# One shared tile for the fillers of a row, and a new written-out order, in a four-layer trunk on one core

## The chip, the cores and the metric

The kernel runs on one core of one Trainium2 chip. The metric is the device time of one execution in microseconds (us). The core's engines work side by side, each through its own queue in order: PE (TensorE, matrix products; PEld is its loading of weights), DVE (VectorE), ACT (ScalarE), POOL (GpSimd) and SP, which here only issues transfers (DMA) from and to the chip's memory.

## The reference

A residual trunk of four layers over 256 tokens of width 1024, each a token mixer followed by a SwiGLU FFN of inner width 2816. Layers 0 and 3 mix with the recurrent RWKV-7 form, layer 1 with stick-breaking attention, layer 2 with sparse attention over 64 selected keys.

```python
for i in range(DEPTH):                     # DEPTH = 4
    kind, j = i % 3, i // 3
    h = rms_norm(x, norm_mix[i])
    if kind == 0:   y, v_layer = rwkv7_time_mix(h, v_first, ...)   # a scan over the tokens, 16 heads of 64
    elif kind == 1: y = stick_breaking_attention(h, sb_w_qkv[j], sb_w_out[j])
    else:           y = dsa_attention(h, ds_w_in[j], ...)
    x = x + y
    x = x + swiglu(rms_norm(x, norm_ffn[i]), ffn_w_gu[i], ffn_w_down[i])
```

All of it is in float32.

## The kernel before

The residual x lies transposed in four tiles `xt` (128 channels x 2 x 256 tokens each). Weights come as 397 pieces of 128 x 1024 float32 (512 KB). Each is loaded into one of three buffers `raw` (`piece`, L639), cast on ACT or DVE to a rounded half `wh`, and DVE forms the rest `wl` = raw − wh; products are then sums of passes with `wh` and `wl`. Where the program takes unsplit float32, as in the sums of squares `ss` and the LoRA products `lora_in`, a matmul instruction shows as two records in the profile.

The first recurrent layer begins like this (`prep_chunk` L732, `rwkv` L890): the four parts of x are loaded; ACT squares them and DVE adds; four matmuls with ones make the sums over channels (`ss`); ACT and DVE make 1/rms of them (`rstda`, `rstdm`, `rstd`). The LoRA input weights, the first 512 KB of `lora`, are scaled on DVE (`mu`, `lora`), and PE multiplies x by them (`lora_in`). When rstd is there, DVE makes the normed h and its mixtures (`pre`, `xm`), these are split into `kx`, and PE starts the key projection (`kp`). A second transfer of 1.5 MB brings the rest of `lora`, which `lw` and `la` read first.

Nothing here is issued in program order. `Plan` records all 6561 operations with their dependencies. The text `ORDER` (L302) holds, packed, the order in which they are issued, the engine of each operation that could run on more than one (801 of them), and the buffer slot of each tile; a search made it, with a planner's costs (`_cost`, L253). `schedule` (L481) unpacks it, and `emit` (L529) issues the operations in that order, each into its engine's queue. All are thereby recorded at one line, L560.

An entry of the order that names no operation is a **filler**: work for PE without use, whose place the search chose. `emit` looks for a PSUM slot that no product holds (`held`) and calls `warmer` with it; `warmer` (L1607) then issues two matmuls (`WARMERS`, L220) of 256 columns of ones in bf16, `warm_x`. Each of the two matmuls takes a new tile `warm_o` in that slot. A slot has one buffer (`bufs=1`), so a new tile in it stands for the end of the one before.

Of the kernel before, what the change touches and what calls it, by code (L numbers as in the profile page):

```python
# [15 lines left out]
F32 = mybir.dt.float32  # L16
# [39 lines left out]
_o = 0  # L56
# [163 lines left out]
WARMERS = 2  # L220
# [87 lines left out]
SA;iomc0Icd(#bMS4_wDlD%R5V>9F>OIN-
5{Ey0cUC*`sd|prIbRko*GrAaOLQDFp%w;Y3^Q@DX+4v7Lf8aSXwxxD`i#xtuu&rDyB>#YOU%W5mmjsvM=~HftXPooLoL}62z%MvIr>i@h?w#>desIQ*IX
~q4e2)nDXn*T`^NRBWeo22D{DiOd==oXib9{G$kIv8e;ssImR`3>f5nFTE#(%;lV!b}V`fly-v5ytR5@G>y9<x8p;!HJ0j4-4-A!ZS64;`dW%aRI<-  # L310
)Pl^rE;Yz$AWevq3+uvj6^^m-
+AtpU6e&D?_$=;#<8EtWPrQ(0_OY3TqbO039cCvQVgc1PUK&`^%fK2knw%S*zVUE+ZnMDb*lr`?=v>f*4EgX%T`xbnceHLWs7weaCT0yE^E)UJFLT5qt$F
MR%ec!U18-;f2qStE!IVr7qwQd$tqb^D?x?X`H<xSvYuiYX3u#HKv_)c40YxZJW>~W3}R5QDa%Z-
0(Tnxi?*&=Y$jAYN;Ey`9x+F86@c<?domUoYc_(gZArc0X?0PPcE^^b75PxhysScHExVtEVtZ6<#c<Kc>_dH>jl$J%r3vR@xL7aF@6NNrJAR(!z=h5lMOf
2;2jM1^ydrbm+>*<jejLN+X8CGlS)fndX$`eiMT6_bGN>YWZ+qM=g2R`<s^Z+b*7|m_HwuCPF0<CAa=}qPJhX%Zig#C|C|cer>H@#WtG@E~s_@8lVd$X8t
O{dKEeN)?q>!hWhbPh!Lq{lU^Vo{3N~o(68A3{^KNI$zsPGUP3PCvQjw6_LWdY(5S_d1JWr+_~G%8DJ4)-
M66O3~JwngG;xKc_D73s4n)xJ_7uOyITfKuxqB@+W6-v$AkuW-N-
;w1uc?i1@H1=~_e4dS_kJt1gR93U{_g3%RSP@io8;66U4zVRjo&&(_eM#L!LJq29sC5%HuEa55eQNq|KXCTfe_<zs&_~$q;UvfSqgMcvF8v@P{mYDHUq7!
g5R*^1_u|a`sE*NaVYfLOQ1mM%R2N^mBU~Vrn2<al{nTO#5<mhCc!cy8zWL*>x6XdWU9eHKK4@sA9`iYdwP^4Q?);#c*fntk-huX4&oRI`WBMGuO_WA%5S
$e4~`9zjz2>DDV8LI^z#R3sp6rnVfLo$W3O~<_4kXh+TaE8dajy35js5ecZZv@5z0x`r|h<H#oQ@fi9<bdX$KnHk>y1+nG$WDqkBp@dhBZz$<ogA14$8sN  # L320
# [48 lines left out]
"""


class Plan:
# [156 lines left out]
    def emit(self, nc, counts, warmer):  # L529
# [15 lines left out]
        for b in left:  # L545
            for o in b.ops:
                of[o].append(b)
        for n, o in enumerate(ops):
            if o is None:
                free = [(at, tag) for tag, (at, b) in held.items() if b is None]  # L550
                if free:
                    warmer(min(free)[1])
                continue
            for b in of[o]:
                left[b].discard(o)
                held[b.slot] = (n, b if left[b] else None)
            if not o.instrs:
                nc.scalar.preload_act_table_set(o.table)
            for method, args, kw in o.instrs:
                getattr(getattr(nc, o.eng), method)(*map(real, args), **{k: real(a) for k, a in kw.items()})  # L560
# [1042 lines left out]

    wx = sb.tile([P, S], BF16, name="warm_x")
    nc.vector.memset(wx, 1.0)
    plan.emit(nc, {"ps": 6, "g": 2, "xm": XMS, "raw": RAWS, "wh": 3, "wl": 3, "t": TS, "t2": 5},
              lambda tag: [nc.tensor.matmul(psum.tile([P, 512], F32, name="warm_o", tag=tag, bufs=1)[:, :S], wx[:, :P], wx, start=True, stop=True)  # L1607
                           for _ in range(WARMERS)])

# [159 lines left out]
```

## Time and profile before

| | us |
|---|---|
| time, median of 3 runs (lowest, highest) | 1365.79 (1365.06, 1367.98) |
| profiled execution | 1365.3 |
| its span, first to last instruction | 1363.5 |
| PE busy | 1353.9 |
| DVE busy | 1131.2 |
| ACT busy | 728.2 |
| PE busy with fillers (46 matmuls) | 16.3 |

The profile shows one execution. Times in it count from the start of the span. A row of a timeline has the start, the duration, the engine, the line, the operation, what it writes and reads, and how many instructions are merged in it; in brackets stands for how long the engine was idle before, and what ended that. `x8` for a float32 product means four instructions. Matmuls overlap in the pipeline, so the distance between starts tells the rate, not the duration.

The stages follow one another on PE: recurrent layer 0 to 196 us, its FFN to 379, stick-breaking to 500, FFN to 678, sparse attention to 820, FFN to 998, recurrent layer 1 to 1177, FFN to the end.

### The profile page before, as it was taken

Reading aid. Unit: us, or ns where it says so; the run is one execution under the profiler, and the core shown is the slowest. Engines: PE = TensorE matmul, PEld = TensorE weight load, DVE = VectorE, ACT = ScalarE, POOL = GpSimd, SP = SyncE. Lnnn points to the kernel's source line nnn. Section 1 sums busy time; section 2 is a strip of 40 time slices with the busy share of each in tenths; the row PEclk is TensorE's granted clock in tenths of the full one; section 3 lists DMA queues with packets and bytes.
Section 4 is the critical chain, followed back from the end, with each engine's and each line's share of the span. In section 5 each row is a group of like instructions: output and inputs, shape, how many; then the busy total and the mean of one; then the engine's idle time right before and its main releaser. Section 6 shows DMA issues by size and latency. Waiting matters only on the chain.

```text
span 1363.5 us, 25718 instructions
## 1 busy us (share of the span) xinstructions
PE 1353.9 (99%) x10380; PEld 1183.0 (87%) x10380; DVE 1131.2 (83%) x1913; ACT 728.2 (53%) x1245; POOL 8.3 (1%) x18
## 2 busy tenths in 40 slices
PE   9999999999999999999999999999999999999998
PEld 5888798888888898888899798888898888988888
DVE  5999799876688899876799989877699997998754
ACT  3765465654344655654346866554148564656532
POOL 0000000000000000000000000000000000000000
PEclk9999999999999999999999999999999999999999
DMA  5524157664655356655646546666653331666554
GB/s 181 169 88 126 34 154 219 200 194 145 186 175 165 113 185 202 203 176 163 199 155 184 157 140 216 204 196 203 187 153 111 111 98 34 199 206 199 174 172 132
DMA packets 62999, 221.89 MB, mean 163 GB/s; under 512 B 7328, under 2 KB 8864, under 8 KB 62624
## 3 DMA queue, kind: packets, MB, share of 16 engines
q1 hardware_dynamic: 62880, 220.25, 52.4%
q8 instruction: 81, 1.33, 0.4%
q14 instruction: 38, 0.31, 0.1%
HBM read 217.08 MB, written 1.05 MB: 160 GB/s over the span
## 4 chain that ended last, share of the span: by engine, by line
PE 98%; DVE 1%; DMA 1%; issue 0%; ACT 0%; DVEq 0%; SPq 0%
PE gate L560 18%; PE up L560 18%; PE dn L560 18%; PE po L560 7%; PE qk L560 6%; PE vp L560 4%; PE rp L560 3%; PE vps L560 3%; PE kp L560 3%; PE z L560 2%; PE warm_o L1607 1%; PE sc L560 1%; PE Y L560 1%; PE cmb L560 1%; PE pg L560 1%; PE attn_o L560 1%
## 5 line engine op out<-in xcount | busy, mean ns | idle before, releaser
L560 DVE TENSOR_TENSOR wl<-raw,wh 128x1024 fp32r<-128x1024 f32 x285 | 347.3, 1221 | 85.3 <-ACT wh L560 82.2
L560 ACT CAST wh<-raw 128x1024 fp32r<-128x1024 f32 x219 | 229.3, 1049 | 179.2 <-PE dn L560 92.4
L560 PE MATMUL dn<-h,wh 128*128 128x512 f32 (+1 forms) x726 | 244.3, 383 | 0.0
L560 PE MATMUL dn<-h,wl 128*128 128x256 f32 x704 | 198.1, 282 | 0.0
L560 PEld LDWEIGHTS dn<-h,wh 128*128 128x128 f32 x726 | 134.7, 188 | 26.9
L560 PE MATMUL up<-xg,wring 128*128 128x512 f32 x704 | 139.8, 336 | 0.0
L560 PE MATMUL gate<-xg,wring 128*128 128x512 f32 x704 | 138.3, 336 | 0.0
L560 PEld LDWEIGHTS dn<-h,wl 128*128 128x128 f32 x704 | 133.0, 189 | 0.0
L560 DVE TENSOR_TENSOR wring<-raw,wring 128x1024 fp32r<-128x1024 f32 x88 | 107.5, 1222 | 28.9 <-ACT wring L560 27.9
L560 PE MATMUL gate<-xg,wh 128*128 128x512 f32 x352 | 126.8, 392 | 0.0
L560 PE MATMUL up<-xg,wh 128*128 128x512 f32 x352 | 126.5, 392 | 0.0
L560 PEld LDWEIGHTS gate<-xg,wring 128*128 128x128 f32 x704 | 107.5, 188 | 14.7
L560 PEld LDWEIGHTS up<-xg,wring 128*128 128x128 f32 x704 | 107.4, 188 | 14.6
L560 ACT CAST wring<-raw 128x1024 fp32r<-128x1024 f32 x76 | 79.9, 1051 | 35.8 <-issue 15.3
L560 PE MATMUL up<-xg,wl 128*128 128x256 f32 x352 | 98.4, 280 | 0.0
L560 PE MATMUL gate<-xg,wl 128*128 128x256 f32 x352 | 98.4, 279 | 0.0
L560 PE MATMUL qk<-xg,wh 128*128 128x256 f32 (+1 forms) x384 | 91.8, 320 | 0.0
L560 PEld LDWEIGHTS up<-xg,wh 128*128 128x128 f32 x352 | 66.1, 188 | 14.5
L560 PEld LDWEIGHTS gate<-xg,wh 128*128 128x128 f32 x352 | 66.1, 188 | 14.5
L560 PE MATMUL qk<-xg,wl 128*128 128x256 f32 x256 | 71.7, 280 | 0.0
L560 PEld LDWEIGHTS qk<-xg,wh 128*128 128x128 f32 x384 | 63.8, 189 | 6.2 <-issue 0.5
L560 ACT COPY gus<-gate 128x256 f32<-128x256 f32 x88 | 32.3, 373 | 68.9 <-PE gate L560 66.8
(325 smaller groups left out, 2663.9 us busy)
## 6 DMA issues: line engine op xcount, KB each, us to landing
raw<-in_wts_dram SPq DMA_DIRECT2D x397, 512.0 KB, 3.8
lora<-in_lora_dram SPq DMA_DIRECT2D x2, 1536.0 KB, 9.0
rhl<-qa SPq DMA_DIRECT2D x32, 64.0 KB, 3.4
xt<-in_xT_dram SPq DMA_DIRECT2D x4, 256.0 KB, 3.6
lora<-in_lora_dram SPq DMA_DIRECT2D x2, 512.0 KB, 5.7
lg<-in_lora_dram SPq DMA_DIRECT2D x8, 128.0 KB, 3.6
inv<-in_id_dram SPq DMA_DIRECT2D x2, 512.0 KB, 4.0
out_dram<-xt SPq DMA_DIRECT2D x3, 256.0 KB, 4.5
```

Of the source, the lines that this page charges most:

```text
L560: getattr(getattr(nc, o.eng), method)(*map(real, args), **{k: real(a) for k, a in kw.items()})
L1607: lambda tag: [nc.tensor.matmul(psum.tile([P, 512], F32, name="warm_o", tag=tag, bufs=1)[:, :S], wx[:, :P], wx, start=True, stop=True) for ...
```

## The change

There are two parts.

**Fillers in a row share one tile.** `emit` keeps the tile of the last filler. The next filler writes the same tile again, as long as no product has taken the slot in between. The two matmuls of one filler share it too. `warmer` takes the tile where it has one.

**A new order.** The packed text is replaced. It keeps all 6561 operations. Unpacked, the two texts compare as follows.

| | before | after |
|---|---|---|
| entries | 6584 | 6595 |
| fillers | 23 | 34 |
| fillers ahead of the first `ss` | 19 | 27 |
| other fillers on PE, in runs | 2, 1, 1 | 1, 1, 2, 1, 2 |
| operations on DVE | 1896 | 1899 |
| operations on ACT | 1208 | 1205 |

The order within the sparse attention layer is the same on every engine. In the two recurrent layers and in stick-breaking attention it changes on PE, DVE, ACT and SP, in the FFNs at their ends, mostly. Operations that change engines: 29 from DVE to ACT and 29 back in recurrent layer 0, 25 and 17 in stick-breaking attention, 21 and 23 in recurrent layer 1, 31 in all in the FFNs. Many buffer slots change.

The head of SP's queue, where the first layer starts:

```
before: xt1 xt0 xt2 xt3 vecs lora(512 KB) raw raw raw raw consts raw lora(1.5 MB) raw raw raw ...
after:  xt0 xt1 xt2 raw vecs xt3 lora(512 KB) raw raw raw lora(1.5 MB) raw raw raw raw raw consts ...
```

On ACT, the cast of the first weight piece moves from behind `rstd` to ahead of the squares of `xt3`, and DVE's split of that piece to ahead of the scaling of `lora`.

```diff
@@ -300,72 +300,75 @@
 ORDER = """
-c-rk+S#KoCab{%XRd-ca-xvELn`iTEcC&eN$>ChfA$NvzXm+*I>{{}!4qLKy*cJ=}h5*}u{9qV<Fkr|Jda(RzKgcisBmM=3U_gJsfFrBAIWwAFOSWWK3oz
...
+c-rk+*>9xVQFqnZzrA<2?cUvXyWMWPSFbZ3d+Zr|#-
...
 """
@@ -545,15 +548,20 @@
         for b in left:
             for o in b.ops:
                 of[o].append(b)
+        filler = None
         for n, o in enumerate(ops):
             if o is None:
                 free = [(at, tag) for tag, (at, b) in held.items() if b is None]
-                if free:
-                    warmer(min(free)[1])
+                if filler is None and free:
+                    filler = min(free)[1], warmer(min(free)[1])
+                if filler is not None:
+                    warmer(*filler)
                 continue
             for b in of[o]:
                 left[b].discard(o)
                 held[b.slot] = (n, b if left[b] else None)
+                if filler is not None and filler[0] == b.slot:
+                    filler = None
             if not o.instrs:
                 nc.scalar.preload_act_table_set(o.table)
@@ -1603,9 +1611,15 @@
     wx = sb.tile([P, S], BF16, name="warm_x")
     nc.vector.memset(wx, 1.0)
+
+    def warmer(tag, t=None):
+        if t is None:
+            return psum.tile([P, 512], F32, name="warm_o", tag=tag, bufs=1)
+        for _ in range(WARMERS):
+            nc.tensor.matmul(t[:, :S], wx[:, :P], wx, start=True, stop=True)
+
     plan.emit(nc, {"ps": 6, "g": 2, "xm": XMS, "raw": RAWS, "wh": 3, "wl": 3, "t": TS, "t2": 5},
-              lambda tag: [nc.tensor.matmul(psum.tile([P, 512], F32, name="warm_o", tag=tag, bufs=1)[:, :S], wx[:, :P], wx, start=True, stop=True)
-                           for _ in range(WARMERS)])
+              warmer)
```

More of the change, by code (lines that the diff above doesn't have):

```diff
@@ L308 @@
[L308 to L320, printed above, removed]
@@ new lines @@
+Ub6zb|cMIR~y@h(to#Q)2cPm}+ouTj=u5XUap*!xlgUH!6E!V$e_M1azAzWTI-Eln|ICTg3(%*!-q!-
+kmsGsD+;*Z@zO|f*@q;jSj$#lU;Cf(ncWGjQd_zmSmeAQD@My~pnqrNHKue)4G;Yg00A@>AhMxc5_aQ^&ld;{4Fj(Bl=j*synzKw|Y>2rK^f_QuP&L_Bc8
++Q?R5bu6%YY&O!0ta;S7&q_`KkVX5JYHEn!uAE;!4`JUaIl29jMzl1#y{o1!f^@bNa$?g&v7uD$2?+s>EF|sqDL5@j~F;<%=;dqpHk>xRVaaZUSV@Nk@+>
+57oLmR)cg5#ikr7WFAyL4oEKfk&*x1Jvu+k=vVNMUJsx4mBzgk5QTm+Coa=`YrM%x)bp6qxL`>~-WP5yfPjKAc=38_(!eL{G!@&@--
+*+n;=+xJ+)52AT&6ZqVMA5`rgI8-<VOT<m&F-
+AQIu@`}Y39pV%He!D%e+~JvknFUW_rw{O@=<22sJC1b;W4U8u^e3R$z3K(Ku4`r0cBku=*i)c*&rajO}<;;S!S;MHS$-
@@ new lines @@
+FFo$6h#!P9sB7tA*_F=7IiH)G6IFqmD!;&UJc}82KgTdr!7>JY4CmIvVkN}F-NO7b**n*HSz!4U=A=s*Oz)*qSiw-OsQHhUl~?q3XOF#51mkQFG~I_iQ53
+V)*|3eyS&o}#$E4A;a@8F6vkx@-
+s?x!*RO(~?G%tMAs}w>e(C5)cRP5?mT|o5C%|@o#&A4fKQA0DTV6&|Kb@b+f5uW=6*W2K;*#c}jPaS9IH~}{=g24EC$Xu10(`;6%wx1j4z&n#}529!*58<
+OM)6nx~70BljTqQv34Xr`ZSr0*}9>GUr=H>1T!y^|R2k3oI6TwrHj1A-a(DCHhbzL}jz_^?)Z37zBx`GoD>VmUO&-
+%uk8gSMel48zG&ln%pJZbqJJ3zOVaW!V#P;e?i5Mzs;4UBm}kGnDBxs_v}n=n3cfNr@4(}@{-
+3LX%n0LN*8A<l>NcwJk@M^=u3bsaN4bzl%PD$}7YVPC;RNu0o)6=EEcf?y3njF0KgSTRx&<Anpmgi)<o#(`ZiX5?*R9GUw>+CwrM=u;vB8SBGQK{KYSavH
@@ new lines @@
+F087jco!Y(857?bjl5OR75m`0%C(<cq9bPep&HH3)fbb@q^+BBh&qE9ED%9NxPRs{hmrw|N)@B!9IK+F&Eltf!_Kv;v>m^ovYS%W;pO98AY$XPuZ4{1q8`
+17iOsV?0_mwc>CY76q|bk@GClhU3CZVH^xy2}cvlv1IZC5sHgtO_VcD3zyIQcHTSR7Kq*E78_xdBiI`;9&~c>>jgb=sRdAhFeGy5oiX=vuI{S9ytnz=^}<
+?tbq39uegMqhGJQ-
+=_*GGe4JzW<cMQ6&&oNL&6*7AFQqUVWFSn1TOUVJ7=rM7%gdzn4;H;f!>iw0S~^;)*WvpOc2cibYpenXo8@u&oli!i^6(48tzl*Gt<m7^;czfO=q+qKJKZ
+?hcndyQKi)W!r`<zw@5#M`<Aaw+M+bKgP7h)B&dHs9eq31b_TMRayWYq1ovp=ecEmSZZehqb$~;&9UdJ3|Lq5A4@LNs)yT`l{90oNmeptD6E4LTz?na^*Z
+i?~a&L|kJ4ubamr)_OoKhVp3Y3cS7KbDK|hk}WH7`+Wc7?ihO_WS)(?}xg-@n*00Qm@bd08i?jx#RFi-L14*xO^L6uj#(Kv*Yf5ac+liZ*CR83?nlH-ADB
@@ new lines @@
+x183dh+U!xclXfMT0FIhFO|CZGO;y`@=C`VQ{py{K+&W}Exti|DqO)9zPMzlB_M(%kk8-
+u30AH$59kJj;O3xPxI?RPUOQ;gLy+x39!;S@vQGorSe_H_OYJnV~h>Wwx4l5hApoNkze6fiHDg$YDW%yhN&>0EONw<IiPVNM&TY>gl@(qt7O@JED@?n{m#
+2(DQm}ih46D*ha$}h`1`BJF_?<}-&1;E?$Alz;=puP`FU#a14HI3zT=|FuorEW(m)PaBlf*1mc5KiZq4+YGNgPbrKq2Jdc+fss%tw9LC<-
+lFfkgpP41c8QU3Mi!t?(c#pnL{RR8H&a?WrH#$H#kb|>wyjlIxajU(}L!txhq-Q5EN5R-
+DpTjMj0JZ7%o#Ba^AVec??8I$UA{Ei?BTnCuA{h+T$3Z&NKtLCefnKxy70_3pKPpA>o;sAmP|zDDg@QQO+~MEI!aNP{o`BIJe>76+&!-
+^Mpc;Ji;b~3uTg3VorK@0TUctC;d?kCu@?rgb$mB02c-
@@ new lines @@
+A*Fn^F@2m4+2Q0*P?T`CQ5bGfL+_So&`d%Kv!FJ-9&{A5jc+i#6ON`1k=@~<-)$m|#DA7wxM5Eg6IXPJx2)9T5|8<n?Q?GYf(iT&!rA!6a4yv<;*-
+pcE(GY!StqlS9>acb@8EUK#UJK@SOD)pm<aB=hxYQ7$9pYQaVZKvB@t_J>gJ}UUCxUy5;_-k+%ie-pa7Ti2GN3a;MmRI}Hk5j6_Gc`Z8#L|mVO0<7Ba+fR
+FLbxEnFM8=PHTNA;Bp<;a$zO$xFbWEiV&EgS0t6+`QM}>3*BCsh=W0-
+WoLxH2mZ6>zaG26ZcMf#nOy`3JsI8}4TPj!CPE&OC7O|h|M!FN`PYCOLky=bQ3ZfZRoiM`*Y$FyHA<PCY@Vk0GWJcB58f61&$T(2pg^mpt>I_KOEP6F@<g
+&6OmBy1sfVTWsj>FDbxK8+;lkKdZ>523Msy;iRG^*^u`JgEl#T<3tRG*aLAzxtK`Ai+!=`;??a8`=e7ih32nE@+;zg}2eT*Qk;9&0%8E4@l3lY#N$H0a0)
@@ new lines @@
+Hz=h2bcT<<?xhAPG4IYn@t&aaL-(=^)J&{3VD%`45b{8ZU>$0;V}F%<thDdKeTS-
+N2;Mc2U6vW;q~N|0qD)qCM3<t|lPm6FCPN9~!7XFfgMhzJf>&&xhWAubzK6CrB^VH^LMgO}E!Ko^nbR7__4NaTpw?_5dv2k3gAmk(XO6}Cev&3Sgp^eE%7
+@phURy86eSvvm?=CrQmKY|W-KC0;I6<BzjH|$GMxkWXkJ0{VEa!S=8hxJpq9MslpC`W%NMGd_o2p;UFA}Eth3;O-
+FU0s+`9;Dszr>86KfmD0Yw}C|Q~8A@1poPJhWR&|{_7IJzra5;=CZU+K#L^6wJ(<}U1(=37T!74)tqO5EfEpKiD=d44RR;4fbB3K&KtIq&e`9*PT3=BGb=
+V?)H1cnM<|O>;iB1!B0y(UItNrHWE@Ie8ko<7NQ*Y@%q~T-lF4UymZx~srQ4kEXSnC_HJ56+jN>e%$lV-
+#80AbDvikv}jgpt8sMrX&;&N*kH%?RwvW`t>G**F-
@@ new lines @@
+l8jO=leY6+MFy97Nr9dPE;vLX1Q+19r~wJ6#g~x*qwi>TTf?4$oq*k<Cc_zq;*WqS<~q#qN57+)OZMQn>kZI{^xZT&VvklG{3>>#-
+C1E@royb%Py?#YstxHfRawB&n*kJ!e*&&=phGn+=H<Kq>ML}`_W*sJQ<~vA8Idv~2mFs!gsv-
+>`?k&5lcJ^!MJ>;Gx+r;Qj)ebZu3Y{w6gjT9J$>kMHB>EsIi-2NBmN$1wEOZV8{a9hu*T<>SvOTGvYKf9X}*$oO9FDH2#_hLR9Jv02Yx709-
+V`ia=cHRsN*`3_g(%8dB$&fbox?r$!$p?ZSHqDqrgNe9X>#OkHg~!c<&71<<Tje0NjJe0C&mYcj$8qU>6=d19%_y-
+i3EyXAH+fI2jM9=jioe<MAOCD+B1l=Egm8s`u8~OVEbpR-gQ_R)+?)RnUNctc<K%E(}UUxj0WxTBLmw@_#WV_AC`RiSPOm{291u@^#l}GOV>;&Q|#~P16=
+HF;!N@8WqK|7^-}cV6pJQR|HTf^2q&|OAjLQ*1Ujh_JTutX#SE@vS0xVd~y;=-TdJU`N&W7jGo~XY1WMn#lZo&EA>>cJD}JF+}gBp2(-n1-
@@ new lines @@
+dY8o?T|U<yU$C8x>ZssnEWz0%Vq9iSjAM5I~ipIs*$F<_J{^EYDb$R7%And`nK=2R4J-
+u#PpME5uhT53ddT9msTMM@(^@<`rsdZ1$>vSB2q(dnz`jjTL~Y)a1-A?=KaAWCm9xI3)u7X|?fZ=$Eie7sqRI;x&_1E`=tf*L1s7W4a<-
+t^m_re1<Nsx7c*I@vGP=Kc)4jm@kbrvC&lTt0yp3?{YRZ=%pR6O<vg?ex?Ta3jMWXfX_I1+ks!1>UCyd>}Rb6S3lE#c)1anYzqLd@BNyAt{Lr`lfh@7(Wl
+3!|70oN{0xbqV$e=Gn;fP6wt?A5q2sjiMO(Aw7J!gc+JK-aLP2Dl@;XXkIpXggh(^%Na<a)LY*<cwf=#T<1;wphlrA(Uq0GiDr-
+z&goJ2B_b9=RWXK`2xE)n8~a>8uaA`Lmx#J-@aR$4l$a_!gtNV<_ev>8rING@m_bdl0B3Qd)ouqZk~*!T<+43WgIBsI8JF12)$I5}F?NH`Z-NMy-jC3|9t
@@ new lines @@
+$tK}rg$RY98MnKRcLA|~u*s>>Z&Jt#w5CZO@##woKx{&0*QedSN;dJ1pNGtzSgb?*GMSMMSM$j%p@@&`a+V-$vQsvhT@IW)r9-qk7CbpGb}30<;zt-CT%r
+xe=8Hj_2-
+uV$e$A#fpfgBF?5#b9IK22oU3(JjDiT=ocEUe}F>4QYT~VuKoH=6^?Q66L0TW#krxlYZwD)mb!~}Bc!Hgvb{(nK1oEJm9HY1MdJkfHp^~v;d#xJLM_3&!Y
+Gs(35ss;sK`bB)0f&$mpB+SNzhQw&LqKKWEP3>Um1zawNleH%xVdY=?FGbQ+3B0c4lqXr8G$x>-
+W<c9I$A+e)T~M?VnIIgYWKNM~VMQ~kL~Jmms+QuO(_30Ob|KBJ`C^E<<^fkmPvY{*ORWlY@HQMdyNXd}m5XBr<M6f0C2kT+;+WVy_6<2TvzP?&|B_6^t4`
+oxI*YfI%%@sG0>Nwoq?2&GoK8G#3d=DJPp~ZUpeqEA&y~k8K`wySqOo@}`&Sk!QN(5e@{JhT@iHDK0nM(=%wk6oR*3Z*E5`nxpmkgs7qSy1w9smKB}<M(#
@@ L369 @@
+%CrhhfODxI=ICPn?GU)vV9n-AVqTU1iBV8h?`z%!fj#yCWNw&MPs{DyB%r22SEE@HFR%L-sXU$%$s6kVj-
+f}(t5eIhmtk|n1vH=mmuM4QhKmU^T8#e$IpZ&%g7jh<TP6(#+afPn<fL61dhBs2zEurrot1U|6{T%n7szLKRpw#!E<>zi$j2>{{^dFD)I
 """
```

68 lines of the change are left out of this document (15 added, 53 removed).

## The prediction

> **What bounds the kernel now.** I read the page first: the busy times and the chain that ended last.
>
> ```profile
> span 1363.5 us, 25718 instructions
> PE 1353.9 (99%) x10380; PEld 1183.0 (87%) x10380; DVE 1131.2 (83%) x1913; ACT 728.2 (53%) x1245; POOL 8.3 (1%) x18
> ...
> PE 98%; DVE 1%; DMA 1%; issue 0%; ACT 0%; DVEq 0%; SPq 0%
> ```
>
> TensorE is the bound, with 9.6 us idle (1363.5 − 1353.9). A reordering that leaves its instructions alone can win only idle time, or PE time in which nothing useful runs. So next: what PE waited for, and the busy time by stretch (columns: length, then busy time and count for PE, PEld, DVE, ACT, POOL; granted clock, DMA share, GB/s).
>
> ```profile
> PE warm_o L1607 <- DVE warm_x L1605: 1.2, 1, 1.2
> PE pS L560 <- DVE Sn L560: 0.7, 2, 0.5
> PE lw L560 <- DMA lora<-in_lora_dram: 0.5, 1, 0.5
> PE vb L560 <- ACT ysq L560: 0.5, 1, 0.5
> ```
>
> ```profile
> 0.00:17.43 17.43, 14.12 (x38) 3.91 (x38) 5.21 (x13) 4.87 (x6) 0.89 (x6) 1.00 0.55 189
> 17.43:27.39 9.96, 9.96 (x40) 8.57 (x41) 5.47 (x11) 5.20 (x8) 0.00 (x0) 1.00 0.13 38
> 27.39:196.00 168.61, 167.04 (x2083) 146.04 (x2082) 155.24 (x311) 100.47 (x181) 3.67 (x5) 1.00 0.39 121
> 196.00:379.00 183.00, 183.00 (x1058) 161.50 (x1057) 144.22 (x202) 91.98 (x139) 0.00 (x0) 1.00 0.61 187
> 379.00:500.00 121.00, 120.92 (x805) 105.37 (x804) 104.35 (x183) 63.45 (x125) 0.40 (x1) 1.00 0.49 154
> 998.00:1177.00 179.00, 177.98 (x2159) 155.03 (x2159) 165.62 (x322) 107.45 (x197) 3.04 (x4) 1.00 0.33 103
> ```
>
> The stretches are: start, lora_in, rest of recurrent layer 0, its FFN, stick-breaking, recurrent layer 1. After 27.39 us PE idles 1.57 us in the first recurrent layer (168.61 − 167.04), 0.08 in stick-breaking, 1.02 in the second: 2.7 us in all. Only the first stretch looks different: there 38 matmuls fill 17.43 us. So, its timeline on PE:
>
> ```profile
> 1.20 16.18 PE L1607 MATMUL warm_o<-warm_x 128*128 128x256 bf16 x38 [1.20 <-DVE warm_x L1605]
> 17.43 3.40 PE L560 MATMUL ss<-sq,ones 128*128 128x256 f32 x8
> 20.68 7.07 PE L560 MATMUL lora_in<-xt,lora 128*128 128x256 f32 x32
> 27.39 0.79 PE L560 MATMUL kp<-kx,wh 128*128 128x256 f32 x2
> ...
> 41.05 9.46 PE L560 MATMUL kp<-kx,ahead 128*128 128x256 f32 x78
> ```
>
> ```profile
> 1.65 0.10 PEld L1607 LDWEIGHTS <-warm_x 128*128 128x128 bf16 x1 [0.32 <-issue]
> ```
>
> The fillers (warm_o) stand 16.23/38 = 0.427 us apart, while a 256-column matmul of kp takes 9.46/78 = 0.12: before each filler's weight load the engine sits 0.32 us on "issue", a wait the profile puts down to nobody. Each of them has a tile of its own. Was PE needed sooner? On ACT and DVE:
>
> ```profile
> 8.20 0.42 ACT L560 ACTIVATE sq<-xt 128x256 f32<-128x256 f32 x1 [2.11 <-DMA xt<-in_xT_dram]
> ...
> 20.88 0.47 ACT L560 ACTIVATE rstda<-ss,eps_rms 128x256 f32<-128x256 f32 x1 [10.96 <-PE ss L560]
> ...
> 22.15 1.03 ACT L560 CAST wh<-raw 128x1024 fp32r<-128x1024 f32 x1
> ```
>
> ```profile
> 8.93 0.42 DVE L560 TENSOR_TENSOR sq<-xt 128x256 f32<-128x256 f32 x1
> 9.95 2.51 DVE L560 TENSOR_TENSOR lora<-lora,mu 128x512 f32<-128x512 f32 x4 [0.60 <-DMA lora<-in_lora_dram]
> ...
> 21.38 0.42 DVE L560 TENSOR_SCALAR rstdm<-ss 128x256 f32<-128x256 f32 x1 [8.92 <-ACT rstda L560]
> ...
> 23.60 1.22 DVE L560 TENSOR_TENSOR wl<-raw,wh 128x1024 fp32r<-128x1024 f32 x1
> ...
> 27.34 0.41 DVE L560 TENSOR_TENSOR kx<-xm,kx 128x256 fp32r<-128x256 f32 x1
> ```
>
> ss had its last input at 9.35 us and began at 17.43: **8.1 us of the start are fillers and nothing else**, with ACT waiting 10.96 us behind them.
>
> **The change, part by part.** The order text, unpacked as `schedule` (L481) unpacks it, has 19 fillers ahead of ss before and 27 after.
>
> 1. *Start fillers.* After, 54 matmuls write one tile. If they stream: the rate doubles once PE has worked densely. ss starts 3.25/8 = 0.41 us apart (17.43 to 20.68), lora_in 6.71/32 = 0.21 (20.68 to 27.39; the same kind, two records to an instruction), a ratio of 1.94, so the switch came some 3.25 us after the first unbroken work, although the clock column says 1.00 throughout. A filler then takes 0.12 warm, 0.23 cold: 14 cold in 3.25 us, 40 warm in 4.8, end at 1.20 + 8.05 = 9.25 us. Never warm: 54 × 0.23, end at 13.6.
>
>    The Trainium skill ("TensorE: Matmul & The Clock Gate", Part 1) lets the clock up only after a busy window of about 3.4 us, and lets the windows run freely, so up to two may pass; the 3.25 us above agree with one. By it, as an estimate, 30 fillers could be cold and the end 10.9.
>
> 2. *ss itself.* The new order issues xT's fourth part behind the first weight piece and the vectors instead of right behind the third, and ACT casts that piece (1.03 us) before the last two squares. SP's queue now:
>
> ```profile
> 0.75 1.81 SPq L560 DMA_DIRECT2D xt<-in_xT_dram  x4
> 2.60 0.43 SPq L560 DMA_DIRECT2D vecs<-in_vecs_dram  x1
> 3.07 0.43 SPq L560 DMA_DIRECT2D lora<-in_lora_dram  x1
> 3.55 21.63 SPq L560 DMA_DIRECT2D raw<-in_wts_dram  x4
> ...
> 27.81 0.43 SPq L560 DMA_DIRECT2D lora<-in_lora_dram  x1
> ```
>
> ```profile
> 27.00:37.00 10.00, 9.47 (x78) 8.99 (x77) 9.92 (x24) 4.56 (x7) 1.13 (x1) 1.00 0.97 346
> ```
>
>    0.65 MB more ahead of it at 346 GB/s is 1.9 us: last square after 10.1, two ACT squares of 0.42 end near 10.6. The cast waits for a piece that is ahead of xT's part, and lies in its shadow. So ss starts at 10.6, between 9.4 (nothing lost) and 13.6 (cold fillers). It is warm: 8 × 0.21 = 1.7, end 12.3.
>
> 3. *lora_in* needs the scaled LoRA weights, ready at 12.46 now (9.95 + 2.51). Their transfer moves behind 0.5 MB more (1.4 us), so the first half is scaled near 12.6 and the rest near 13.9, faster than PE reads it. lora_in runs 12.6 to 19.3. DVE meanwhile goes from ss to the first kx: 27.75 − 20.83 = 6.9 us now, less the 1.2 us weight split that moved ahead of it; kx stands at about 18.1. So **kp starts at 19.3 instead of 27.39: 8.1 us earlier**; by the bounds 9.6 (ss at 9.4) or 5.4 (ss at 13.6).
>
> 4. *Does the rest follow?* After kp's start PE, DVE and SP do the same work in both orders. In 27 to 37 us DVE is busy 9.92 of 10 and the DMA engines 97%, so neither could be squeezed, but both are free earlier: DVE does nothing from 12.5 to 21.4, and DMA carries 38 GB/s in 17.43 to 27.39. The large LoRA transfer, issued at 27.81 behind waits for weight buffers, is issued after the fourth weight piece in the new order; it passes the constants and one weight piece, which then land up to 4.3 us (1.5 MB at 346 GB/s) later against it, but in a time when DMA is idle now. It also ends the 0.5 us for which PE waits for it now. The first constants move back behind five weight pieces; their first user on PE is kss, 40 us on:
>
> ```profile
> L560 PE MATMUL kss<-ksq,consts x8: 590/592/595, 71.6 to 80.9; 128*128 128x512 f32 x8
> ```
>
> 5. *Other fillers:* 4 before, in 3 runs; 7 after, in 5.
>
> ```profile
> 153.17 1.26 PE L1607 MATMUL warm_o<-warm_x 128*128 128x256 bf16 x4
> ...
> 154.58 0.41 PE L560 MATMUL xu<-QC,XT 64*64 64x64 f32 x7
> ```
>
> ```profile
> 1130.31 0.61 PE L1607 MATMUL warm_o<-warm_x 128*128 128x256 bf16 x2
> 1130.98 1.01 PEld L560 LDWEIGHTS cmb<-xd,SB 32*64 32x64 f32 x32 [0.56 <-PE warm_o L1607]
> ```
>
>    A run of one costs 0.67 us, the run of two 1.41: 2.75 in all. After, streamed, a run of one saves some 0.2 (0.45), a further filler costs 0.24: 5 × 0.45 + 2 × 0.24 = 2.7. I take 0; if the old runs covered waits and the new ones do not, +2.7, and −2.7 the other way round.
>
> 6. *The order of the three layers.* PE's instructions are the same. 29 operations go from DVE to ACT and 29 back in layer 0, 25 and 17 in stick-breaking, 21 and 23 in layer 1: DVE's sums hardly move and stay below the stretch (155 of 169, 104 of 121, 166 of 179), so PE hides them; without that cover each costs at most a cast of 1.0 us. At best the new order removes the 2.7 us of PE idle, at worst each waiting place adds about 0.35 (pS: 0.7 in 2). I take −0.8 (the LoRA wait and a little), from −2.7 to +5.
>
> Sum: −8.1 + 0 − 0.8 = **−8.9**, span 1354.6. The profiled execution took 1365.3 us, 1.8 more than its span, and the median of the runs lies 0.5 above it: 1354.6 + 1.8 + 0.5 = **1357 us**. Its own range is 1353.5 to 1360.5: 9.6 instead of 8.1 at the start and all 2.7 us of idle gained below (1.5 + 1.9), 5.4 instead of 8.1 and 0.8 not gained above (2.7 + 0.8).
>
> **Rivals.**
>
> - *The start is held up by something else* (the fourth part of xT, or fillers that stay cold). For: xT is issued later. Against: 3.3 MB move in the first stretch (189 GB/s × 17.43 us), of which xT is 1 MB. Gain 5.4 or less: 1360.5 to 1363.
> - *The waits in the layers go too.* 2.7 us of idle and part of the fillers' 2.7: 1365.8 − 8.1 − 2.7 − 2.2 = 1353, and down to 1350. For: the layers were ordered anew. Against: PE idles so little that a search has hardly anything to find.
> - *Slower: the change does not do what it says.* If the wait before each filler comes from writing the same bank and not from the tile's release, 54 × 0.427 = 23.1 us, end at 24.3, everything 6.8 us later: 1372.6. It decides from a spacing of 16.23/54 = 0.30 us. For: "issue" names no releaser. Against: kp's matmuls write one bank after another without any wait, though they accumulate.
> - *The new order loses in the layers what the start wins.* 23 new waits of 0.35 us, or DVE late in a recurrent layer, where it is busy 92%: 1363 to 1369. For: over 140 of some 335 DVE operations of each recurrent layer move. Against: the old order shows three such waits in 1363 us, beside the first filler's.
>
> **How the numbers follow.** Forecast 0.66, held-up start 0.12, more gain 0.08, fillers still waiting 0.07, lost in the layers 0.07. 0.2% (2.7 us) is about what a measurement tells from no change. Below 1363.1: 0.66 + 0.12 + 0.08 = 0.86. The last case splits mostly into "same" (0.06), the fourth is slower (0.08 with what is left). 1352.5 to 1363.5 leaves out the fourth, most of the fifth and half of the third, about 0.16.
>
> **What would show it.** The new timeline on PE: 54 fillers less than 0.25 us apart, ss near 10.6 and warm from its first record (under 2 us for 8), lora_in done near 19.3, kp 8 us earlier. ACT's wait before rstda shrinks from 10.96 to about 2. Later landmarks, such as the start of the first dn, shifted by the same 8 to 9 us:
>
> ```profile
> 318.36 61.03 PE dn L560 x352
> ```
>
> A shift that shrinks from layer to layer shows part 6 wrong, one that grows the third case. Fillers 0.4 us apart would make the prediction wrong at its root; so would an ss that starts after 14 us.

## The result, and the profile after

| | before | after |
|---|---|---|
| median of the runs, us (lowest, highest) | 1366.88 (1365.06, 1368.37) | 1356.72 (1356.41, 1357.60) |
| ratio, with its 95% interval | | 0.9927 (0.991 to 0.9944) |
| profiled execution, us | 1365.3 | 1356.47 |
| its span, us | 1363.5 | 1354.7 |

The change makes the kernel faster: 8.8 us by the profiled executions, 10.2 us by the medians. The two differ because executions of the kernel before spread more, from 1364.5 to 1373.5 us over all comparisons below, half of them at a lower mean TensorE clock, while those of the changed kernel stay within 1355.8 to 1357.9. The forecast had put the chance on faster, at 1357 us.

The page of the kernel after, its span and busy times:

```profile
span 1354.7 us, 25715 instructions
PE 1347.6 (99%) x10402; PEld 1185.3 (87%) x10402; DVE 1135.6 (84%) x1916; ACT 721.5 (53%) x1241; POOL 8.3 (1%) x18
```

PE is busy 6.3 us less (1353.9 before), though it issues 22 instructions more: the fillers were added, and yet cost less. Its idle time fell from 9.6 to 7.1 us (1354.7 − 1347.6). The start of its timeline, in the columns of the prediction:

```profile
1.20 8.53 PE L1619 MATMUL warm_o<-warm_x 128*128 128x256 bf16 x54 [1.20 <-DVE warm_x L1613]
...
9.78 1.99 PE L568 MATMUL ss<-sq,ones 128*128 128x256 f32 x8
...
11.81 0.47 ACT L568 ACTIVATE rstda<-ss,eps_rms 128x256 f32<-128x256 f32 x1 [1.63 <-PE ss L568]
12.07 7.17 PE L568 MATMUL lora_in<-xt,lora 128*128 128x256 f32 x32 [0.29 <-DVE lora L568]
...
18.89 0.59 PE L568 MATMUL kp<-kx,wh 128*128 128x256 f32 x2
19.32 0.28 PE L568 MATMUL kp<-kx,wl 128*128 128x256 f32 x1
```

54 fillers now stand 8.53/54 = 0.158 us apart, where 38 stood 0.427 apart. ss begins at 9.78 instead of 17.43, ACT waits 1.63 us for it instead of 10.96, and kp begins at 18.89 instead of 27.39: 8.5 us earlier. Whether this lasts is read from the down products of the FFNs. Their tile view names the first start and the last. Before, then after:

```profile
L560 PE MATMUL dn<-h,wh x726: 277/390/392, 318.2 to 1359.5; 128*128 128x512 f32 x171, 128*128 128x256 f32 x11
```

```profile
L568 PE MATMUL dn<-h,wh x726: 277/390/392, 309.1 to 1350.7; 128*128 128x512 f32 x171, 128*128 128x256 f32 x11
```

The first starts 9.1 us earlier, the last 8.8. Nearly all of the gain is there after the first 19 us; from there to the first dn 0.6 are added, and from the first dn to the last 0.3 are given back. What PE waits for after:

```profile
PE pS L568 <- DVE Sn L568: 0.6, 1, 0.6
PE vps L568 <- DVE qk L568: 0.3, 1, 0.3
PE gate L568 <- DVE gus L568: 0.3, 1, 0.3
PE lora_in L568 <- DVE lora L568: 0.3, 1, 0.3
PE qu L568 <- PE xu L568: 0.2, 1, 0.2
```

Beside the first filler's, before had 1.7 us of such waits in three places (pS, lw, vb). After has 1.7 us in five (0.6 + 0.3 + 0.3 + 0.3 + 0.2). The wait for the large LoRA transfer is gone, and so is vb's; four new ones came.

### The profile page after: what moved, and what is told of

Read it like the earlier page. It is cut to its first block, busy times and chain, and to the rows that moved or that the text cites. A ratio compares the mean times of both kernels' runs of the same rounds, so it can differ in the third digit from the quotient of the medians.

```text
span 1354.7 us, 25715 instructions
## 1 busy us (share of the span) xinstructions
PE 1347.6 (99%) x10402; PEld 1185.3 (87%) x10402; DVE 1135.6 (84%) x1916; ACT 721.5 (53%) x1241; POOL 8.3 (1%) x18
## 4 chain that ended last, share of the span: by engine, by line
PE 95%; DVE 3%; DMA 1%; issue 1%; ACT 0%; SPq 0%; DVEq 0%; ACTq 0%
PE dn L568 18%; PE gate L568 16%; PE up L568 16%; PE po L568 7%; PE qk L568 7%; PE vp L568 4%; PE kp L568 3%; PE rp L568 3%; PE vps L568 3%; PE z L568 2%; PE sc L568 1%; PE Y L568 1%; PE lora_in L568 1%; PE pg L568 1%; PE cmb L568 1%; DMA raw<-in_wts_dram 1%
## 5 line engine op out<-in xcount | busy, mean ns | idle before, releaser
L568 ACT CAST wh<-raw 128x1024 fp32r<-128x1024 f32 x216 | 225.9, 1047 | 176.4 <-PE dn L568 99.8
L568 ACT CAST wring<-raw 128x1024 fp32r<-128x1024 f32 x73 | 76.7, 1050 | 32.8 <-issue 15.0
L568 DVE CAST wh<-raw 128x1024 fp32r<-128x1024 f32 x69 | 47.6, 690 | 27.9 <-PE dn L568 16.9
```

## The experiments

The theory on trial: the shared tile takes away a wait before each filler, this brings the start forward, and the written-out order adds almost nothing. Its rivals: the order makes the gain, or the wait comes from something else than the tile. Fillers compute nothing, so the kernels below that leave some out still compute everything. The four kernels of the first group ran beside one another, and so did those of the second and of the third.

### 1. The shared tile alone

The changed kernel with the order text of before (23 fillers, 19 of them at the start):

```diff
 ORDER = """
-c-rk+*>9xVQFqnZzrA<2?cUvXyWMWPSFbZ3d+Zr|#-
+c-rk+S#KoCab{%XRd-ca-xvELn`iTEcC&eN$>ChfA$NvzXm+*I>{{}!4qLKy*cJ=}h5*}u{9qV<Fkr|Jda(RzKgcisBmM=3U_gJsfFrBAIWwAFOSWWK3oz
...
```

> The old order with the new, shared filler tile: only the fillers' part of the change. Theory A (the start was held up by fillers that waited for each other, and sharing the tile is nearly the whole gain): the 38 start fillers end before 8.5 us instead of 17.4, ss starts at about 9.4 when its last input is there, kp near 18.5, the whole 1357.5 to 1358.5 us. Theory B (the new order brings the gain, its head of the queues above all): kp starts after 21 us and the time stays above 1361.

1354.44 us (1352.97 to 1354.80), ratio 0.990 (0.9885 to 0.9915), span 1352.5: **one part alone gives more than the whole change**, and some 3 us more than theory A had put on it. PE's timeline, and the rows of the down products and of the last layer's fillers:

```profile
1.20 5.99 PE L1616 MATMUL warm_o<-warm_x 128*128 128x256 bf16 x38 [1.20 <-DVE warm_x L1610]
...
10.54 7.34 PE L565 MATMUL lora_in<-xt,lora 128*128 128x256 f32 x32 [0.59 <-DVE lora L565]
17.54 0.47 PE L565 MATMUL kp<-kx,wh 128*128 128x256 f32 x1
18.28 0.39 PE L565 MATMUL kp<-kx,wh 128*128 128x256 f32 x1 [0.28 <-DVE kx L565]
18.50 0.28 PE L565 MATMUL kp<-kx,wl 128*128 128x256 f32 x1
...
1117.43 0.39 PE L1616 MATMUL warm_o<-warm_x 128*128 128x256 bf16 x2
1117.88 0.69 PE L565 MATMUL cmb<-XT,zs 32*32 32x32 f32 x32
```

```profile
L565 PE MATMUL dn<-h,wh x726: 277/390/392, 307.4 to 1348.5; 128*128 128x512 f32 x171, 128*128 128x256 f32 x11
```

38 fillers stream at 0.158 us (5.99/38), the same pace as the 54. kp's first product is at 17.54, 1.35 us ahead of the changed kernel; its second waits for `kx`, so that the third is only 0.82 us ahead (18.50 against 19.32). A run of one filler takes 0.45 us (1117.43 to 1117.88), as the prediction had put it, against 0.67 before.

So the new order costs 2.2 us (1354.7 − 1352.5). Where, is seen when the two kernels are cut at the same two products, kp and the first dn. The windows of the changed kernel, then those of the old order with the shared tile (length, then busy time and count for PE, PEld, DVE, ACT, POOL, then clock and DMA):

```profile
18.89:309.07 290.18, 289.62 (x2793) 254.15 (x2791) 262.79 (x462) 164.47 (x285) 4.36 (x5) 1.00 0.47 146
309.07:1350.70 1041.63, 1040.29 (x7519) 917.09 (x7518) 860.34 (x1426) 546.44 (x941) 3.03 (x7) 1.00 0.54 167
```

```profile
17.54:307.43 289.89, 288.74 (x2788) 253.57 (x2787) 261.37 (x463) 169.90 (x291) 3.69 (x5) 1.00 0.49 153
307.43:1348.50 1041.07, 1039.96 (x7517) 916.64 (x7516) 858.94 (x1426) 549.11 (x941) 3.64 (x7) 1.00 0.54 167
```

1.35 us are lost before kp's first product, 0.29 from there to the first dn (290.18 − 289.89), 0.56 in all the rest (1041.63 − 1041.07). Cut at kp's third product, where neither kernel waits any more, it is 0.82 before, 0.82 from there to the first dn and 0.56 after it. In the middle stretch the new order does find idle time: PE idles 0.56 us (290.18 − 289.62) instead of 1.15. But it is busy 0.88 us longer, and most of that are fillers, here the groups of the two kernels in that stretch:

```profile
L1619 PE MATMUL warm_o<-warm_x 128*128 128x256 bf16 x8 | 1.4, 276 | 0.0
```

```profile
L1616 PE MATMUL warm_o<-warm_x 128*128 128x256 bf16 x4 | 0.6, 275 | 0.0
```

### 2. The new order alone

The kernel before with the new order text: each filler matmul has its own tile again.

> The new order with the old fillers, each matmul in a tile of its own. Theory A: 54 fillers 0.427 us apart end at 24.3 us, ss starts there, some 14.5 us later than with the shared tile and cold, so about 1371 to 1373 us, slower than the kernel before. Theory B: at most 1362.

1374.51 us (1373.90 to 1375.42), ratio 1.0047 (1.0031 to 1.0064): slower than before.

```profile
1.20 23.01 PE L1610 MATMUL warm_o<-warm_x 128*128 128x256 bf16 x54 [1.20 <-DVE warm_x L1608]
24.26 3.78 PE L563 MATMUL ss<-sq,ones 128*128 128x256 f32 x8
...
35.54 0.58 PE L563 MATMUL kp<-kx,wh 128*128 128x256 f32 x2
```

The fillers stand 23.06/54 = 0.427 us apart and end at 24.3, the figure that the prediction had for its rival "the change does not do what it says" (54 × 0.427). The new order has eight more fillers at the start than the old one and pays for each.

### 3. No fillers at the start

The kernel before, its 19 start fillers left out:

```diff
         for n, o in enumerate(ops):
+            if o is None and n < 100:
+                continue
             if o is None:
```

> The old order and old fillers, but none of the 19 ahead of the first ss. Theory A: ss starts near 9.4 us, cold (3.4 us for 8 records), the clock rises one to two windows of some 3.3 us later, kp starts at 20 to 21.5, in all 1359.5 to 1361 us: most of the gain without any filler. If the fillers' time was covered by another wait (a rival to A: a transfer that ends near 17 us), ss would still start after 15 us and the time stay at 1366.

1356.24 us (1355.94 to 1357.48), ratio 0.9917 (0.9902 to 0.9932).

```profile
6.87 3.78 PE L562 MATMUL ss<-sq,ones 128*128 128x256 f32 x8 [6.87 <-DVE sq L562]
10.45 7.33 PE L562 MATMUL lora_in<-xt,lora 128*128 128x256 f32 x32
17.42 0.87 PE L562 MATMUL kp<-kx,wh 128*128 128x256 f32 x2
```

Without any start filler kp begins at 17.42, with 38 fast ones at 17.54 (and in experiment 4 at 16.96: two executions with the same head lie 0.6 us apart). The expectation, kp at 20 or later and 1359.5 us or more, took a cold start to cost far more than it does. ss runs cold here (3.78 us for its 8 records, against 1.99 in the changed kernel), but lora_in, which in experiment 1 waits 0.59 us for the scaled LoRA weights, is not later for it. **Up to kp the start fillers buy nothing that shows; the change wins by no longer paying for them.** Over the whole kernel this run is slower than its nearest relative, experiment 4, which has the same later fillers: all four executions took 1355.9 us or more, there all four 1355.7 or less. In the profiled one 1.3 us are a wait of PE at 149 us that the profile puts down to "issue", of which more below; whether the other three had it is not shown.

### 4. Own tiles, but the free slots in turn

The kernel before, where each start filler's matmul takes a new tile in the next free slot instead of always the same one:

```diff
-                    warmer(min(free)[1])
+                    if n < 100:
+                        free.sort()
+                        warmer([free[(WARMERS * fills + i) % len(free)][1] for i in range(WARMERS)])
```

> The old order, each filler matmul at the start still in a tile of its own, but the six free slots are taken in turn. If the wait is for the end of the matmul that held the slot before (theory A1), it is long over after six turns: spacing 0.23 cold and 0.12 warm, about 1358 us as with the shared tile. If a new tile costs its 0.32 us by itself, whatever the slot (A2), spacing stays at 0.427 and the time at 1366.

1354.74 us (1353.62 to 1355.66), ratio 0.9904 (0.9889 to 0.9919).

```profile
1.19 6.70 PE L1613 MATMUL warm_o<-warm_x 128*128 128x256 bf16 x38 [1.19 <-DVE warm_x L1611]
```

0.176 us apart (6.70/38), and the time is some 3 us below the 1358 expected, as in experiment 1. A new tile for each matmul is nearly free when another slot is there for it, so the wait of 0.32 us was for the end of the matmul that had held the slot before. Sharing the tile and taking slots in turn remove it alike.

### 5. The new order with the old head

The changed kernel with the fourth part of xT loaded behind the third again, its squares ahead of the first weight cast, the weight split behind the LoRA scaling, the second weight piece and the large LoRA transfer behind that, and 19 start fillers (`move` puts one operation ahead of another, 0, or behind it, 1):

```diff
+        move(3, 2, 1)
+        move(22, 67, 0)
+        move(23, 67, 0)
+        move(68, 35, 1)
+        move(69, 68, 1)
+        move(30, 69, 1)
+        for k in [n for n, o in enumerate(ops[:100]) if o is None][19:][::-1]:
+            ops.pop(k)
```

> The new order and shared tile, but the head of the first layer undone: xT's fourth part loaded right behind the third, its two squares ahead of the cast of the first weight piece, that piece's DVE split behind the scaling of the LoRA weights (with the two transfers that wait for it), 19 fillers instead of 27. Theory H (the new order loses 1.35 us of its 2.2 against the old order with shared fillers in this head): lora_in starts at about 10.5 us instead of 12.07, kp near 17.6, and all later marks 1.3 us earlier: about 1355.4 us. Rival: kp waits for the weight split and the kx chain on DVE, which now come later, kp stays at 18.9 and the time at 1356.7.

1358.16 us (1357.24 to 1359.36), ratio 0.993 (0.9915 to 0.9945): slower than the changed kernel by 1.3 us of span (1356.0), not faster. The theory that the head's three moves cost the 1.35 us failed in this form.

```profile
10.42 2.50 DVE L583 TENSOR_TENSOR lora<-lora,mu 128x512 f32<-128x512 f32 x4 [0.84 <-DMA lora<-in_lora_dram]
...
11.77 7.17 PE L583 MATMUL lora_in<-xt,lora 128*128 128x256 f32 x32 [1.59 <-DVE lora L583]
18.99 0.84 PE L583 MATMUL kp<-kx,wh 128*128 128x256 f32 x2
```

lora_in began only 0.30 us earlier, and kp 0.10 later: it waits 1.59 us for DVE, and DVE for the LoRA transfer, which stands behind a weight piece here as in the changed kernel. The new order also scales the four quarters of the LoRA weights in another sequence, and lora_in's first matmul waits for two of them. Behind kp's start it loses more: its first product with `ahead` starts at 25.85, in the changed kernel at 24.74, and in between PE waits for the weight split (`wl`) that the edit moved back, as the rival had it. One thing the edit leaves as it is: the new order loads xt0 first, the old one xt1. In all six traces with the new order's text, this one too, ACT's first square starts at 5.00 to 5.50 us; in the eight with the old text at 3.84 to 4.45. No run swapped these two transfers.

### 6. No fillers at all

Experiment 1 without its 23 fillers (`if o is None: continue`).

> The old order without any filler. Theory F (the fillers only take PE time): some 1.6 us less than with shared fillers, the 4 later ones gone and the start limited by the LoRA scaling at 10.5 us either way: 1352 to 1353.5 us. Rival (the fillers hold the clock up): the clock drops to half somewhere in the stretch of small matmuls of a recurrent layer, each lost window of some 3.4 us costs 1.7 to 3.4 us: 1356 or more.

1353.40 us (1352.08 to 1357.46), ratio 0.9901 (0.9883 to 0.992). Four of six executions took 1352.1 to 1353.5, two took 1357.0 and 1357.5. The profiled one is of the latter. A stop in its timeline of the last recurrent layer, then the window from 2.7 us behind this stop on (clock third from the end):

```profile
1113.71 0.59 PE L567 MATMUL cmb<-xd,SB 32*64 32x32 f32 x13 [0.53 <-issue]
```

```profile
1116.40:1126.70 10.30, 10.30 (x202) 9.23 (x204) 4.46 (x12) 1.57 (x6) 0.00 (x0) 0.50 0.01 3
```

For 10.3 us TensorE got half its clock, from 2.7 us after PE had stood still for 0.53 us at "issue". So both came: theory F in four executions, the rival in two. At half the clock 10.3 us hold work of 5.2 at least, an estimate; so this one place can carry the 4 us between the two groups of executions.

### 7. The new order without its start fillers

The edit of experiment 3 in the changed kernel.

> The new order and shared tile without the 27 fillers ahead of ss. If warmth at the start is worth nothing because the scaled LoRA weights come later anyway (12.0 us): ss is cold but done by 12.5, kp within 0.6 us of 18.9, 1356.5 to 1357.3 us. If it is worth what it speeds up: ss ends 1.6 us later and part of lora_in runs at half rate, 1358.5 to 1360.

1356.91 us (1356.20 to 1357.47), ratio 0.9919 (0.9905 to 0.9934): as the changed kernel.

```profile
18.75 0.58 PE L570 MATMUL kp<-kx,wh 128*128 128x256 f32 x2
```

kp at 18.75 without the 27 start fillers, 18.89 with them. They buy nothing that shows in the new order either.

### 8. The new order without its seven later fillers

As above, with `n >= 100`.

> The new order and shared tile with the start fillers but without the 7 later ones. If they only take PE time (0.45 us a run and 0.24 a further one): 2.7 us less, 1354 us. If they stand in time that PE would wait anyway, as the prediction took half of them to do: 1355.5 to 1356.7. If they hold the clock up: 1358 or more.

1355.12 us (1353.70 to 1355.66), ratio 0.9905 (0.9889 to 0.9922), span 1353.0.

```profile
L570 PE MATMUL dn<-h,wh x726: 277/390/392, 307.9 to 1349.0; 128*128 128x512 f32 x171, 128*128 128x256 f32 x11
```

The first dn comes 1.2 us earlier than in the changed kernel, the last 1.7. So the seven fillers take some 1.7 us of PE, not the 2.7 expected, and bring nothing back in this execution; none of the six executions had a mean clock below 0.999.

### 9. The old order with the new head

Experiment 1 with the head of the new order moved in: the first weight piece, vecs, xt3 and the LoRA load behind xt2, in this sequence, that piece's cast ahead of the squares of xt3, its split ahead of the LoRA scaling, and the scaling's quarters swapped in pairs:

```diff
+        move(66, 2, 1)
+        move(6, 66, 1)
+        move(3, 6, 1)
+        move(29, 3, 1)
+        move(67, 22, 0)
+        move(68, 33, 0)
+        move(34, 33, 0)
+        move(36, 35, 0)
```

> The old order with the shared tile, and into it the new order's head: first weight piece loaded ahead of the vectors, xT's fourth part and the LoRA weights; its cast ahead of the last squares; its split ahead of the LoRA scaling; the two halves of each scaling in the new order's sequence (second operand first). Theory H2 (the new order loses its 1.35 us at the start because lora_in's first operand is scaled later: one split and one product more ahead of it, and a later transfer): lora_in starts at about 12.0 us instead of 10.54, kp near 18.8 and all marks 1.2 to 1.4 us later than with the shared tile alone, about 1355.7 us. Rival (the loss lies in how the new order goes on after kp's start): kp at most 0.4 us later, 1354.4 to 1354.8.

1354.90 us (1354.41 to 1357.63), ratio 0.9913 (0.9893 to 0.9933), span 1353.2. Timeline, then the tile views of rp and of the down products:

```profile
11.42 7.17 PE L580 MATMUL lora_in<-xt,lora 128*128 128x256 f32 x32 [1.52 <-DVE lora L580]
18.24 0.59 PE L580 MATMUL kp<-kx,wh 128*128 128x256 f32 x2
18.67 0.28 PE L580 MATMUL kp<-kx,wl 128*128 128x256 f32 x1
...
147.61 0.22 PE L580 MATMUL qu<-UV,QC 128*64 128x64 f32 x1 [0.73 <-issue]
```

```profile
L580 PE MATMUL rp<-prx,wh x256: 277/280/684, 43.3 to 1060.4; 128*128 128x256 f32 x128
L580 PE MATMUL dn<-h,wh x726: 277/390/392, 308.2 to 1349.1; 128*128 128x512 f32 x171, 128*128 128x256 f32 x11
```

The new head delays lora_in by 0.88 us and kp's first product by 0.70 against experiment 1, half of what H2 had. But kp's third product comes only 0.17 us later (18.67 against 18.50), because in experiment 1 the second waits for `kx` and here it does not; rp starts 0.3 us later (43.0 there). Both are less than the 0.6 us between two executions of one head. The 0.8 us at the first dn hold a wait of 0.73 at "issue", at 147.6 us, which has nothing to do with the head. In the old order these moves thus cost at most some 0.3 us in the end. The changed kernel's lora_in and kp lie another 0.65 us behind these (12.07 against 11.42, 18.89 against 18.24); the swap of xt0 and xt1, which this edit leaves out too, is an untested candidate for that.

### 10. The old order with only the last layer's two fillers

Experiment 1 without the 19 at the start and the two in recurrent layer 0 (`n < 1000`).

> The old order with the shared tile and only the two fillers in the last recurrent layer: none at the start, none in the first recurrent layer. If these two hold the clock up there and the others only take PE time: 0.63 us less than with all shared fillers at the start, 0.77 less in layer 0, about 1353 us, and no execution with the clock at half around 1117 us, as without any filler in two of six. Rival: the clock drops in some executions all the same, 1357 in them.

1353.74 us (1352.69 to 1357.97), ratio 0.9907 (0.9884 to 0.993), span 1352.2; one execution of six took 1357.97, at a mean granted clock of 0.996, as the rival had it.

```profile
L567 PE MATMUL dn<-h,wh x726: 277/390/396, 306.6 to 1348.1; 128*128 128x512 f32 x171, 128*128 128x256 f32 x11
```

The first dn is 0.8 us earlier than in experiment 1, with kp's third product at the same time (18.50 in both): that is what the two fillers of recurrent layer 0 take in the old order, against some 1.1 for the new order's (1.2, of which 0.15 are there at kp already: 19.17 in experiment 8, 19.32 in the changed kernel). Without fillers in that layer the new order is still 1.3 us behind at the first dn (307.9 against 306.6). Half of that, 0.67, is there at kp (19.17 against 18.50); the other half is lost behind it, in recurrent layer 0.

### 11 and 12. Both kernels again, unaltered

> The changed kernel unaltered, beside the others on one chip: 1356.4 to 1357.6 us as before, some 2 us above the old order with the shared tile, and no execution with a lower granted clock.

> The kernel before unaltered, for its profile. Its times spread from 1364.5 to 1370.6 us, with mean granted clocks from 1.0 to 0.996. If the clock goes to half in a recurrent layer as it did without fillers, a profile at 0.996 shows some 10 us at half there and marks that jump by 4 us at that place. If it is the start, the marks differ from the first products on.

The changed kernel: 1356.47 us (1355.77 to 1357.85), ratio 0.9923 (0.9904 to 0.9942). The kernel before: 1368.79 us (1364.45 to 1370.71), ratio 1.0002 (0.9986 to 1.0019) to the runs of before beside it. Its profiled execution took 1370.71 us, 5.4 more than the one of the prediction. The timeline of PE in recurrent layer 0, then the window at half the clock (1.00 on both sides of it):

```profile
156.68 1.15 PE L560 MATMUL qu<-UV,QC 128*64 128x64 f32 x31
160.21 0.27 PE L560 MATMUL qu<-UV,QC 128*64 128x64 f32 x1 [2.38 <-issue]
...
168.32 1.13 PE L560 MATMUL vb<-ysq,consts 128*128 128x512 f32 x2
```

```profile
159.40:166.20 6.80, 5.99 (x115) 5.44 (x116) 2.99 (x8) 0.76 (x2) 0.00 (x0) 0.50 0.01 2
```

In the execution of the prediction this vb starts at 162.98. PE stops for 2.38 us in the middle of a row of 32 matmuls, waiting for nothing that the profile names (the last section says what it most likely lacked). Within the stop, at 159.4 us, the clock goes to half for 6.8 us, and vb is 5.3 us late. So the medians' 10.2 us hold the traces' 8.8 and, most likely, a share of this. Of the 43 executions of the kernel before in these comparisons, 22 had a mean clock of 0.998 or less (1367.4 us and more); of 32 with the new order, none. That is not the new order's doing alone: of the 18 with the old order in experiments 1, 3, 4 and 9, none had it either.

## Why the prediction was right, step by step

- **The wait before each filler, and its end (part 1): right.** Own tiles bring it back (experiment 2), another slot removes it as the shared tile does (4). The fillers ended at 9.73, where 9.25 was forecast, because the clock came up later than in the 3.25 us read from before. The fillers' count by stretch in the changed kernel, on PE (length, busy, count, clock, DMA):

```profile
1.20:3.20 2.00, 2.00 (x10) 1.00 0.57 128
3.20:5.20 2.00, 2.00 (x11) 1.00 1.09 248
5.20:7.20 2.00, 2.00 (x16) 1.00 0.83 309
7.20:9.70 2.50, 2.50 (x24) 1.00 1.03 391
```

  The pace doubles within the third stretch, some 4 to 6 us after the first filler. The clock column shows 1.00 there, as it did before, because the trace's list of granted clocks begins only with the entry for full speed. That entry is at 6.27 us here, 5.1 us after the first filler, and 3.4 to 5.6 us after it in the seven traces with fast start fillers; so the end of the fillers, 9.7 us here, changes from execution to execution. The Trainium skill ("TensorE: Matmul & The Clock Gate", Part 1) asks for one busy window of about 3.4 us and lets the windows run freely, so that up to two may pass. The traces agree, and the end here lies between the forecast 9.25 and the 10.9 us estimated from that page.

- **ss and lora_in (parts 2, 3): right in mechanism, each somewhat earlier than forecast.** ss started at 9.78 for 10.6, lora_in at 12.07 for 12.6, kp at 18.89 for 19.3: 8.5 us gained for 8.1. The estimate made ss wait for the last square; PE started on its first inputs while ACT still squared (`sq` runs to 10.18):

```profile
9.46 0.72 ACT L568 ACTIVATE sq<-xt 128x256 f32<-128x256 f32 x2
```

- **The rest follows (part 4): right.** The shift of kp, 8.5, is 9.1 at the first dn and 8.8 at the last. The LoRA wait of lw is gone, and the constants, moved back, delay nobody: no product waits for them in the list above.

- **Other fillers (part 5): 0 was taken, and the bounds hold.** The price of a run of one was right (0.45 us, as measured), but the new runs cost PE 1.7 us in all (experiment 8) instead of 2.7, where the old ones cost 2.75 by their rows: some −1 instead of 0. What the step also missed is that neither set was needed for the time of the undisturbed execution.

- **The order of the layers (part 6): −0.8 was too good.** From kp to the end the whole change gave 0.3 us (8.8 − 8.5), and that holds the 1 us just said that the fillers there cost less; the order itself then lost some 0.7 (an estimate from these two). Nor was the new order's price at the start seen: part 2 and 3 counted its moves only against the 8 us of fillers, and never asked what the old head would do with a streaming filler. It would have been at kp's first product 1.35 us sooner, at its third 0.8. So 8.9 against 8.8 is closer than the working deserves: a head 0.4 better and layers 0.5 worse than put down cancel, and that is luck. The mechanism of the head, which is nearly all of the gain, is not.

- **The rivals.** Fillers still waiting: refuted by the spacing, and made real in experiment 2 (1374.5 us, for 1372.6). Held-up start: lora_in does wait for the LoRA weights, but 0.29 us, and the gain of 8.5 is no case of 5.4. More gain in the layers: refuted, the waits there sum to 1.7 us as before. Lost in the layers: in kind it is there, 0.82 + 0.56 us behind kp's third product against the shared tile alone, far below its 6 us and more. (Its "three such waits" of the old order are four, in three places: pS waits twice.)

What stays open: which move makes the new order later at kp, as the swap of xt0 and xt1 was not tried, and what it loses behind kp beside its fillers. Recurrent layer 0 goes on in another sequence there, and no run took that sequence apart.

The old order with the shared tile (experiment 1) is the better kernel: its four executions have spans of 1351.2 to 1353.0 us, ten of the changed kernel 1354.0 to 1355.9. Leaving out all fillers gives the lowest median (1353.40): it takes another microsecond in most executions and loses four in some. Four executions are few to say that experiment 1 never does.

## What to carry to other kernels

Look at the pace of work that is there only to keep an engine warm: if its spacing is not that of the same work elsewhere, it waits, and the cheapest cure may be one tile for all of it, or none of it at all. When two edits come together, price each against the other's result, not against the kernel before: here one edit was worth 11 us and the other −2. Compare kernels at the same products (kp, first dn, last dn) in two traces; a difference then has a place, and one execution's stall does not pass for an effect. Take a mark behind which neither kernel waits: kp's first product was 1.35 us ahead, its third 0.82. And look how far the same mark lies apart in two executions before a few tenths are read as an effect.

## What the hardware showed that was not expected

- **Fillers 0.427 us apart did not raise the clock.** In the kernel before they ran from 1.20 us on, each weight load after 0.32 us of waiting, and ss was still cold 16 us later (0.41 us apart); in experiment 2 it was so 23 us later. In the changed kernel, at 0.158 us apart, the pace doubled after 4 to 6 us.
- **PE can stop at "issue" for 0.5 to 2.4 us** in the middle of a row of matmuls. Three executions with the old order's text did so within some 40 matmuls of one another in recurrent layer 0 (2.38, 1.28 and 0.73 us in experiments 12, 3 and 9), and others with the same order not at all.
- **The stops stand where PE's instructions come in.** Section 3 of the page of the kernel before has a queue whose packets carry instructions:

```profile
q8 instruction: 81, 1.33, 0.4%
```

  Its 81 packets have 16 KB each. PE has 20890 records in that trace (matmuls, weight loads, semaphore waits), some 258 to a packet, so the queue is taken for PE's, at 256 a packet. Counted in the traces, all four stops come after a number of records that is 193 more than a multiple of 256, and end soon after the end of the packet of that number:

| experiment | PE's records ahead of the stop | packet of that number ends, us | PE goes on, us |
|---|---|---|---|
| 12 | 3265 = 12 × 256 + 193 | 12th: 158.58 | 160.21 |
| 3 | 3265 = 12 × 256 + 193 | 12th: 148.07 | 149.40 |
| 9 | 3265 = 12 × 256 + 193 | 12th: 146.28 | 147.61 |
| 6 | 16833 = 65 × 256 + 193 | 65th: 1112.39 | 1113.71 |

  In none of the fourteen traces does PE pass such a count sooner than 1.2 us after that packet. Experiment 3, which has 38 matmuls and their weight loads less ahead of it, stops at another product and at the same count. In the execution of the prediction the 12th packet ended at 154.09, 4.5 us earlier than in experiment 12, and there is no stop. So PE most likely had no further instruction to run. Why a packet comes late, no run shows.
- **Half the clock for 6.8 to 10.3 us came with two of these stops** (2.38 us in experiment 12, 0.53 us in experiment 6), not with the other two (1.28 and 0.73 us). The Trainium skill ("TensorE: Matmul & The Clock Gate", Part 1) puts the fall after an idle window of about 3.4 us. The traces do not agree: both stops were shorter, and the clock fell 1.6 us after the longer one began and 2.7 us after the shorter one had ended. Whether the later fillers guard against the fall, the counts do not settle: 3 of 12 executions had a lower mean clock in experiments 6 and 10, none of six in experiment 8, which has none of them either, half of those of the kernel before, which has four, and none of the 18 in experiments 1, 3, 4 and 9, which have these four too.
